# The gate matmuls of a recurrence as four 64x64 quadrants of the array, with a row-swapped copy of their input

## The chip, the cores and the metric

One core of one Trainium2 chip runs the whole kernel in one launch. The metric is the device time of that launch in microseconds (us). A core has a tensor engine (PE; its weight loads are PEld), a vector engine (DVE), a scalar engine (ACT), GpSimd (POOL) and a sync engine (SP); each works through its own list of instructions in order. Data comes and goes by DMA, issued from SP, ACT or POOL.

## The reference

One layer of a hybrid network: windowed attention and a gated linear recurrence side by side, then a mixture of 16 experts. There are 1024 latent tokens and 256 context tokens, 1280 in all. The part that matters here is the recurrence on 512 channels, in both directions of time (d = 0, 1):

```python
def block_diag_linear(x, w, b):            # 8 blocks of 64 x 64
    xb = x.reshape(x.shape[:-1] + (LRU_BLOCKS, LRU_BLOCK_DIM))
    return jnp.einsum('blnd,nde->blne', xb, w).reshape(x.shape) + b

def lru_coeffs(xc, w_r, b_r, w_i, b_i, lam):
    r = jax.nn.sigmoid(block_diag_linear(xc, w_r, b_r).astype(jnp.float32))
    i = jax.nn.sigmoid(block_diag_linear(xc, w_i, b_i).astype(jnp.float32))
    log_a = -LRU_C * r * jax.nn.softplus(-lam.astype(jnp.float32))
    a = jnp.exp(log_a)
    mult = jnp.sqrt(-jnp.expm1(2.0 * log_a))
    return a, mult * i * xc.astype(jnp.float32)
```

`xc` is the input after a width-4 convolution in time. The two gates r and i are the subject: each is a product with a block-diagonal matrix whose blocks are 64x64. Then h[t] = a[t] h[t-1] + b[t] is scanned forwards and backwards, and both are added.

## The kernel before

The stages follow one another: modulation vectors and the normalised input, transposed; projections for keys, values and the recurrence's input; the recurrence; a gate branch and the stacks of the keys; attention by blocks of 128 queries, with output projection and router of the block before; routing; 16 experts, whose weights stream from memory. Everything is float32; large matmuls are split into two float32r parts, the gates' matmuls are plain float32, which PE runs as two passes for each matmul of the program.

In the recurrence, channels lie on the 128 partitions and tokens in a row. The 512 channels are four channel tiles, t = 3, 2, 1, 0, of two 64-channel blocks each. `XR` (lines 359 to 361) holds five slots of [128, 1286]: `XR[0]` is a tile of its own, `XR0` (`xr_655` in the lists of instructions), the other four are parts of one tile (`xr`). `conv(t)` (line 467) reads slot t and writes slot t + 1, in the order 3, 2, 1, 0; so the last convolution, `conv(0)`, reads `XR[0]`, and after it that slot is free until `k_stack` (line 561) uses it as scratch.

`gate_weights(t)` (line 457) clears a [128, 2, 2, 128] tile and loads two 64x64 blocks for each gate and direction onto its diagonal. `lru_tile(t)` (line 480) then does, for each direction and gate, one matmul of 256 columns into a PSUM tile `pgatec` and two of 512 columns into `pgate`, and ACT takes them through tanh (the sigmoid) into a `gate` tile; four such tiles exist. ACT computes exp and tanh of the r gates, after a table load their square root; DVE multiplies and scans (lines 503 to 517). The next tile's first tanh writes into a `gate` tile that the scans have read (line 511).

Between the tiles' steps stand five steps each of the query projection (line 547: `proj`, 24 matmuls of 256 columns, with an ACT copy `qb` behind each). A scheduler puts the instructions of each engine in order ahead of time by its own estimate of when each is ready; the order is then fixed. PSUM is handed out by tags: `pS` has two buffers of 1024 columns, `pO` two single ones of 512 in turn.

Of the kernel before, what the change touches and what calls it, by code (L numbers as in the profile page):

```python
# [8 lines left out]
F32 = mybir.dt.float32  # L9
# [9 lines left out]
D = 1024  # L19
# [3 lines left out]
KT = 8  # L23
# [25 lines left out]
def _body(tc, nc, A, out, dbg, top):  # L49
# [35 lines left out]
    def act(*a, **kw):  # L85
        """an activation whose table set matters: these keep their order on the engine"""
        if last_act[0] is None:
            i = nc.scalar.activation(*a, **kw)
        else:
            with tc.issue_after(last_act[0].ins):  # L90
                i = nc.scalar.activation(*a, **kw)  # L91
        last_act[0] = i
        return i
# [4 lines left out]
    def warm(n, after=None):  # L98
        """keeps the tensor engine's clock up while it waits"""
# [52 lines left out]
    # softplus(-lam) = max(-lam, 0) + log1p(exp(-|lam|)); log1p(e) = 2 atanh(e / (2 + e))  # L152
# [22 lines left out]
    # sigmoid(z + b) = (1 + tanh(z / 2 + b / 2)) / 2  # L175
# [18 lines left out]
    def ada_chunk(n):  # L194
        """[4 groups x (16 rows of c, 16 of c_ctx), 512] of columns n*512.., in SBUF"""
# [15 lines left out]
    gcol = const.tile([128, 40], F32, name="gcol")       # g1, sh2, sc2, g2, (1 + sc2) * norm2_g  # L211

    def ada_col(n):
        """half of one of g1, sh2, sc2, g2 as columns; the half before is finished first"""
# [40 lines left out]
    def projT(hi, lo, segs):  # L255
        """channel rows: [128 channels, tokens]"""
# [8 lines left out]
    AB = const.tile([128, 2, 8, 2], F32, name="ab")      # (scale, shift), k tile, (lat, ctx)  # L265
    a0 = pool(S_a0, "a0", 2)
    a0x = pool(S_a0, "a0x", 6)
    xT = a0.tile([128, KT, 768], F32, name="xT", bufs=1)      # [ctx 256 | lat 512]
# [24 lines left out]
    def ada_half(h):  # L293
        """scale and shift of half of the channels"""
# [64 lines left out]
    XR14 = pxr.tile([128, 4, NT + 6], F32, name="xr")    # slots 1 to 4; slot 0  # L359
    XR0 = pxr.tile([128, NT + 6], F32, name="xr0")  # L360
    XR = [XR0] + [XR14[:, i] for i in range(4)]
    XC0, XL0 = 0, NCTX + 3                               # [2 | ctx | 1 | 2 | lat | 1]
# [9 lines left out]
    def rope_tables(nm, after=None):  # L372
        """weights of the norm; cos and sin tables with them folded in"""
# [16 lines left out]
    def proj(wg, tt):  # L390
        """token rows: [128 tokens, 256 columns]"""
# [9 lines left out]
    def norm_rope(x, nh, b, tabs_):  # L401
        """x: [128, nh, 64], in place; b: latent block, or None (no rope)"""
# [54 lines left out]
    def gate_weights(t):  # L457
        """block-diagonal [128, (gate, direction), 128] of the channel tile"""
        WG = pl.tile([128, 2, 2, 128], F32, name="wg", bufs=2)
        nc.vector.memset(WG, 0.0)  # L460
        for g, nm in ((0, "lru_w_r"), (1, "lru_w_i")):
            for s in range(2):
                nc.gpsimd.dma_start(WG[s * 64:(s + 1) * 64, g, :, s * 64:(s + 1) * 64],
                                    A[nm][0, :, 2 * t + s].rearrange("d i j -> i d j"))
        return WG

    def conv(t):
        """into slot t + 1, whose input is used up"""
# [11 lines left out]
    def lru_tile(t):  # L480
# [4 lines left out]
        R, I, As = [], [], []  # L485
        for d in range(2):
            for gi, nm, lst in ((0, "b_r", R), (1, "b_i", I)):
                g = pl.tile([128, NT], F32, name="gate", bufs=4)
                ps = pS("pgate")
                po = pO("pgatec")[:, :256]  # L490
                mm(po, WG[:, gi, d, :], xc[:, 0:256], True, True)
                for hh in range(2):
                    mm(ps[:, hh * 512:(hh + 1) * 512], WG[:, gi, d, :], xc[:, 256 + hh * 512:768 + hh * 512], True, True)
                act(g[:, 0:256], po, AF.Tanh, scale=0.5, bias=hb[:, gi, d * 4 + t:d * 4 + t + 1])
                act(g[:, 256:NT], ps, AF.Tanh, scale=0.5, bias=hb[:, gi, d * 4 + t:d * 4 + t + 1])
# [35 lines left out]
    # the router with the second norm's scale in its rows, and its shift's share as a row  # L531
# [75 lines left out]
    S_wo, S_wr, S_cs, S_att = (ExitStack() for _ in range(4))  # L607
    WO = []                                              # (hi, lo) of the attention's rows, of the recurrence's rows
# [27 lines left out]
    def q_stack(b):  # L636
        """[128 (hi, lo), head, 128]; heads 2i: (hi, lo), heads 2i + 1: (lo, hi)"""
# [11 lines left out]
    def scores(b, kv, i, qst):  # L649
        """heads kv * 4 + i and kv * 4 + 2 + i of 128 queries: negated scores, then their exponentials"""  # L650
# [5 lines left out]
        # keys: the window, then the context; for the last block the other way round  # L656
# [38 lines left out]
    def attn_out(b, kv, i, pe, ktiles, mx):  # L695
# [20 lines left out]
        # [(head pair, d), (head of the pair, query)]  # L716
        nc.scalar.activation(QB[b][:, kv * 256 + i * 128:kv * 256 + (i + 1) * 128], po, AF.Copy)

    y7 = QBQ[1].rearrange("p a b -> p (a b)")[:, 0:D]         # the last block's share of the recurrence, over queries used up
# [522 lines left out]
```

## Time and profile before

| | |
|---|---|
| timed runs | 1186.73, 1188.15 and 1192.13 us; median 1188.15 |
| span of the profiled execution, first to last instruction | 1185.1 us; no time of its own is listed, the median of the timed runs lies 3.05 us above it |
| PE | 1091.7 us busy, 92% |
| DVE | 946.1 us, 80% |
| ACT | 792.2 us, 67% |
| POOL | 148.6 us, 13% |
| chain that ended last | PE 68%, DVE 12%, issue 7%, ACT 7%, DMA 4% |
| TensorE clock granted, mean of the span | 0.972 |

All rows below are of this one execution. Times count from the first instruction. A busy PE is a modelled figure: matmuls are pipelined, and a matmul's listed duration is longer than the distance to the next one. The rate of matmuls is read from the starts. The recurrence with the steps between it lies at about 175 to 294 us of the span.

### The profile page before, as it was taken

Reading aid. Unit: us, or ns where it says so; the run is one execution under the profiler, and the core shown is the slowest. Engines: PE = TensorE matmul, PEld = TensorE weight load, DVE = VectorE, ACT = ScalarE, POOL = GpSimd, SP = SyncE. Lnnn points to the kernel's source line nnn. Section 1 sums busy time; section 2 is a strip of 40 time slices with the busy share of each in tenths; the row PEclk is TensorE's granted clock in tenths of the full one; section 3 lists DMA queues with packets and bytes.
Section 4 is the critical chain, followed back from the end, with each engine's and each line's share of the span. In section 5 each row is a group of like instructions: output and inputs, shape, how many; then the busy total and the mean of one; then the engine's idle time right before and its main releaser. Section 6 shows DMA issues by size and latency. Waiting matters only on the chain.

```text
span 1185.1 us, 17663 instructions
## 1 busy us (share of the span) xinstructions
PE 1091.7 (92%) x6481; PEld 876.0 (74%) x6481; DVE 946.1 (80%) x1577; ACT 792.2 (67%) x1159; POOL 148.6 (13%) x216
## 2 busy tenths in 40 slices
PE   3889999899799999999299999999999999999996
PEld 1568787667678888877187888888888888887774
DVE  3664557678795585867988999999999999989885
ACT  3652127666385666664268888888888888887873
POOL 2031110111300000000010111011111011110001
PEclk9999999899889999999699999999999999999998
DMA  9857720102141112116889999999999999999932
GB/s 293 293 175 239 236 64 5 40 1 69 37 108 54 55 54 89 55 54 235 334 300 342 342 382 399 382 391 388 384 381 402 383 394 380 383 377 355 359 101 36
DMA packets 97678, 277.14 MB, mean 234 GB/s; under 512 B 6060, under 2 KB 38088, under 8 KB 97592
## 3 DMA queue, kind: packets, MB, share of 16 engines
q1 hardware_dynamic: 90944, 255.87, 57.7%
q0 software_dynamic: 6000, 20.01, 6.8%
q8 instruction: 51, 0.84, 0.3%
q14 instruction: 35, 0.29, 0.1%
q10 hardware_dynamic: 648, 0.13, 0.1%
HBM read 259.21 MB, written 16.79 MB: 233 GB/s over the span
## 4 chain that ended last, share of the span: by engine, by line
PE 68%; DVE 12%; issue 7%; ACT 7%; DMA 4%; POOL 1%; SPq 0%; POOLq 0%; ACTq 0%; DVEq 0%
PE pu L96 14%; PE pg L96 14%; PE pd L96 13%; PE py L96 7%; PE pxr L96 3%; PE pav L713 3%; PE pscore L96 3%; PE pPT L703 3%; DVE mlo L1066 2%; DMA wada<-in_w_ada_dram 2%; ACT gate L91 2%; PE pproj L96 1%; PE pada L203 1%; PE pT L1107 1%; DVE gate L507 1%
## 5 line engine op out<-in xcount | busy, mean ns | idle before, releaser
L1066 DVE TENSOR_TENSOR mlo<-mraw,mhi 128x1024 fp32r<-128x1024 f32 x384 | 448.1, 1217 | 24.5 <-ACT mhi L1063 23.1
L1063 ACT ACTIVATE mhi<-mraw 128x1024 fp32r<-128x1024 f32 x384 | 397.7, 1064 | 75.4 <-PE pg L96 29.0
L96 PE MATMUL pg<-mlo,xsh 128*128 128x512 f32 x256 | 81.9, 401 | 1.4 <-DVE mlo L1066 1.4
L96 PE MATMUL pg<-mhi,xsh 128*128 128x512 f32 x256 | 80.9, 397 | 0.4 <-ACT xsh L1117 0.3
L96 PE MATMUL pu<-mlo,xsh 128*128 128x512 f32 x256 | 80.2, 394 | 0.8 <-DVE mlo L1066 0.5
L96 PE MATMUL pu<-mhi,xsh 128*128 128x512 f32 x256 | 80.8, 390 | 0.0
L96 PE MATMUL pg<-mhi,xsl 128*128 128x512 f32 x256 | 80.4, 395 | 0.0
L96 PE MATMUL pu<-mhi,xsl 128*128 128x512 f32 x256 | 79.1, 390 | 0.0
L96 PE MATMUL pd<-mlo,hdh 128*128 128x512 f32 x240 | 76.0, 398 | 2.4 <-DVE mlo L1066 2.4
L96 PE MATMUL pd<-mhi,hdh 128*128 128x512 f32 x240 | 76.3, 399 | 0.0
L96 PE MATMUL pd<-mhi,hdl 128*128 128x512 f32 x240 | 74.2, 390 | 0.0
L1156 POOL DMA_INDIRECT out_dram<-ys,idx x16 | 49.8, 3113 | 164.2 <-DVE ys L1154 164.2
L1094 POOL DMA_INDIRECT xs<-xh_dram,idx x16 | 21.4, 1335 | 373.0 <-ACT mhi L1063 317.2
L1116 ACT ACTIVATE xs<-pT,gcol 128x128 f32<-128x128 f32 x124 | 46.9, 462 | 26.2 <-PE pT L1107 26.2
L91 ACT ACTIVATE sc<-sc,mx 128x641 f32<-128x641 f32 (+1 forms) x64 | 50.9, 798 | 15.7 <-DVE mx L677 15.7
L96 PE MATMUL pproj<-wlo,hh 128*128 128x256 f32 x192 | 55.5, 289 | 4.4 <-DVE wlo L243 4.4
L677 DVE CUSTOM_DVE_ANT_0 sc<-pscore,kn,nsink 128x640 f32<-128x640 f32 (+1 forms) x64 | 53.4, 842 | 6.0 <-PE pscore L96 5.8
L96 PE MATMUL pproj<-whi,hh 128*128 128x256 f32 x192 | 57.5, 300 | 0.6 <-ACT gate L91 0.6
L709 ACT ACTIVATE pt<-pPT 128x512 f32<-128x512 f32 (+1 forms) x88 | 44.0, 533 | 18.7 <-PE pPT L703 17.6
L96 PEld LDWEIGHTS pu<-mlo,xsh 128*128 128x128 f32 x256 | 47.1, 188 | 12.6 <-DVE mlo L1066 3.5
L96 PEld LDWEIGHTS pg<-mhi,xsl 128*128 128x128 f32 x256 | 48.6, 190 | 10.6
L96 PEld LDWEIGHTS pg<-mlo,xsh 128*128 128x128 f32 x256 | 46.2, 189 | 13.5 <-DVE mlo L1066 4.6
(329 smaller groups left out, 2444.7 us busy)
## 6 DMA issues: line engine op xcount, KB each, us to landing
mraw<-in_w_gate_dram SPq DMA_DIRECT2D x64, 1024.0 KB, 7.6
mraw<-in_w_up_dram SPq DMA_DIRECT2D x64, 1024.0 KB, 9.3
mraw<-in_w_down_dram SPq DMA_DIRECT2D x63, 1024.0 KB, 9.0
wada<-in_w_ada_dram SPq DMA_DIRECT2D x48, 512.0 KB, 5.8
win<-in_w_in_dram SPq DMA_DIRECT2D x7, 1024.0 KB, 5.4
xt<-in_x_dram SPq DMA_DIRECT2D x8, 512.0 KB, 4.3
xa<-in_x_dram SPq DMA_DIRECT2D x8, 512.0 KB, 3.8
out_dram<-xa SPq DMA_DIRECT2D x8, 512.0 KB, 2.7
```

The source lines that it names most:

```text
L91: i = nc.scalar.activation(*a, **kw)
L96: nc.tensor.matmul(o, l, r, start=start, stop=stop)
L203: nc.tensor.matmul(po[32 * j:32 * j + 32, q * 256:(q + 1) * 256], cst[:, half * 4 + j, :], w[:, j, :], start=(half == 0), stop=(half == 1) ...
L677: nc.vector.tensor_tensor_reduce(out=sb[:, :ntot], in0=ps[:, n0:n0 + ntot], in1=mk, scale=-0.125, scalar=nsink[:, h:h + 1], op0=OP.add, op ...
L703: nc.tensor.transpose(p[:, 2 * j + s, :], pe[s][:, (j0 + j) * 128:(j0 + j + 1) * 128], ident)
L709: nc.scalar.activation(dst, src, AF.Copy)
L713: nc.tensor.matmul(po[s * 64:(s + 1) * 64, :], V[:, kt, kv * 64:(kv + 1) * 64], pt[:, j, s], start=(j == 0), stop=(j == nk - 1), skip_grou ...
L1063: nc.scalar.activation(hi, raw[:, j], AF.Copy)
L1066: nc.vector.tensor_tensor(lo, raw[:, j], hi, op=OP.subtract)
L1094: g = nc.gpsimd.indirect_dma_start(out=xs, out_offset=None, in_=xh_dram, in_offset=bass.IndirectOffsetOnAxis(ap=idx[:, :1], axis=0))
L1116: nc.scalar.activation(xf[:, k], p[:, i], AF.Identity, scale=A_, bias=B_)
L1156: nc.gpsimd.indirect_dma_start(out=out_rows, out_offset=bass.IndirectOffsetOnAxis(ap=idx[:, :1], axis=0), in_=ys, in_offset=None, compute_ ...
```

## The change

The weights of a channel tile are no longer laid out as a 128x128 block-diagonal matrix with zeros. The tile `wg` is now [128, 2, 2, 64]: the r gate's blocks lie in partitions 0 to 63, the i gate's in 64 to 127. A matmul takes a 64x64 block at one of four places of the array, (gate, half of the output channels); its input must lie on the gate's 64 partitions. For the half of the channels whose input lies on the other 64 partitions there is a copy `xsw` of the tile's input with the halves of the partitions exchanged. It is written by two DMAs from POOL's queue, in the slot `XR[0]`.

Names in the diff: `xc` is the convolved input of the tile, `hd` the 64-channel block, `gi` the gate, `tile_position` the first row and column in the array.

```diff
     def gate_weights(t):
-        WG = pl.tile([128, 2, 2, 128], F32, name="wg", bufs=2)
-        nc.vector.memset(WG, 0.0)
+        WG = pl.tile([128, 2, 2, 64], F32, name="wg", bufs=2)
         for g, nm in ((0, "lru_w_r"), (1, "lru_w_i")):
             for s in range(2):
-                nc.gpsimd.dma_start(WG[s * 64:(s + 1) * 64, g, :, s * 64:(s + 1) * 64],
-                                    A[nm][0, :, 2 * t + s].rearrange("d i j -> i d j"))
+                nc.gpsimd.dma_start(WG[g * 64:(g + 1) * 64, s], A[nm][0, :, 2 * t + s].rearrange("d i j -> i d j"))
         return WG
 
+    xsw = XR0[:, 0:NT]
...
         xc = XR[t + 1][:, 0:NT]
         R, I, As = [], [], []
+        for h in range(2):
+            nc.gpsimd.dma_start(xsw[h * 64:(h + 1) * 64], xc[(1 - h) * 64:(2 - h) * 64])
         for d in range(2):
-            for gi, nm, lst in ((0, "b_r", R), (1, "b_i", I)):
+            ps = [pS("pgate") for _ in range(2)]
+            po = [pO("pgatec")[:, :256] for _ in range(2)]
+            for outs, c0, n in ((po, 0, 256), ([p_[:, 0:512] for p_ in ps], 256, 512), ([p_[:, 512:1024] for p_ in ps], 768, 512)):
+                for hd in range(2):
+                    for gi in range(2):
+                        r = slice(gi * 64, (gi + 1) * 64)
+                        src = xc if hd == gi else xsw
+                        nc.tensor.matmul(outs[gi][hd * 64:(hd + 1) * 64, :], WG[r, hd, d, :], src[r, c0:c0 + n],
+                                         start=True, stop=True, skip_group_check=True, tile_position=(gi * 64, hd * 64))
+            for gi, lst in ((0, R), (1, I)):
                 g = pl.tile([128, NT], F32, name="gate", bufs=4)
-                ps = pS("pgate")
-                po = pO("pgatec")[:, :256]
-                mm(po, WG[:, gi, d, :], xc[:, 0:256], True, True)
-                for hh in range(2):
-                    mm(ps[:, hh * 512:(hh + 1) * 512], WG[:, gi, d, :], xc[:, 256 + hh * 512:768 + hh * 512], True, True)
-                act(g[:, 0:256], po, AF.Tanh, scale=0.5, bias=hb[:, gi, d * 4 + t:d * 4 + t + 1])
-                act(g[:, 256:NT], ps, AF.Tanh, scale=0.5, bias=hb[:, gi, d * 4 + t:d * 4 + t + 1])
+                act(g[:, 0:256], po[gi], AF.Tanh, scale=0.5, bias=hb[:, gi, d * 4 + t:d * 4 + t + 1])
+                act(g[:, 256:NT], ps[gi], AF.Tanh, scale=0.5, bias=hb[:, gi, d * 4 + t:d * 4 + t + 1])
                 lst.append(g)
```

What the scheduler makes of it is shown at three places. The first is PE at the first channel tile, right behind `pbrow`; here its first direction, before (`pgatec_1721` with `pgate_1720` is one gate, `pgatec_1729` with `pgate_1728` the other):

```order
L96 MATMUL pgatec_1721<-xr_654,wg_1485 128x256 [waits DMASW3_49,DMASW2_49,DVE_49]
L96 MATMUL pgate_1720<-xr_654,wg_1485 128x512 [waits Activation_49]
L96 MATMUL pgate_1720<-xr_654,wg_1485 128x512
L96 MATMUL pgatec_1729<-xr_654,wg_1485 128x256 [waits DMASW5_49,DMASW4_49,DVE_49]
L96 MATMUL pgate_1728<-xr_654,wg_1485 128x512 [waits Activation_49]
L96 MATMUL pgate_1728<-xr_654,wg_1485 128x512
```

And the same direction now (`xr0_655` is the exchanged copy; 1721 and 1719 belong to the gate r, 1722 and 1720 to the gate i):

```order
L497 MATMUL pgatec_1721<-xr_654,wg_1485 64x256 [waits DMASW2_49]
L497 MATMUL pgate_1719<-xr_654,wg_1485 64x512 [waits Activation_49]
L497 MATMUL pgatec_1721<-xr0_655,wg_1485 64x256 [waits DMASW3_49,DMASW2_49]
L497 MATMUL pgate_1719<-xr0_655,wg_1485 64x512 [waits Activation_49]
L497 MATMUL pgate_1719<-xr_654,wg_1485 64x512
L497 MATMUL pgatec_1722<-xr0_655,wg_1485 64x256 [waits DMASW4_49,DMASW3_49,DVE_49]
L497 MATMUL pgatec_1722<-xr_654,wg_1485 64x256 [waits DMASW5_49]
L497 MATMUL pgate_1720<-xr0_655,wg_1485 64x512 [waits PE_49]
L497 MATMUL pgate_1720<-xr_654,wg_1485 64x512
L497 MATMUL pgate_1720<-xr0_655,wg_1485 64x512
L497 MATMUL pgate_1719<-xr0_655,wg_1485 64x512
L497 MATMUL pgate_1720<-xr_654,wg_1485 64x512
```

Six matmuls became twelve, the two gates are interleaved, and the third instruction waits for the first exchanged copy, the sixth for the second. In both orders the second direction stands right behind, and only behind that the query projections (`pproj`).

The second place is POOL, from the first weights of the gates on (`wg`: weights; `xr_655<-xr`: the copies). Before, and behind it now:

```order
L463 DMA wg<-in_lru_w_r_dram 64x2x64 x2
L463 DMA wg<-in_lru_w_i_dram 64x2x64 x2
L463 DMA wg<-in_lru_w_r_dram 64x2x64 x2
L463 DMA wg<-in_lru_w_i_dram 64x2x64 x2
L463 DMA wg<-in_lru_w_r_dram 64x2x64 x2
```

```order
L462 DMA wg<-in_lru_w_i_dram 64x2x64 x2
L488 DMA xr_655<-xr 64x1280 x3
L462 DMA wg<-in_lru_w_r_dram 64x2x64 x2
L462 DMA wg<-in_lru_w_i_dram 64x2x64 x2
L488 DMA xr_655<-xr 64x1280 x2
```

Two of the first three copies are the first channel tile's; they wait for the last instruction of `conv(0)`, which reads the slot that they write. The others wait for the matmuls of the tile before.

The third place is ACT ahead of the third channel tile (t = 1). Before:

```order
L552 ACTIVATE qb<-pproj 128x256
L404 ACTIVATE nrsq<-qb 128x512
L552 ACTIVATE qb<-pproj 128x256
L91 ACT_TABLE_LOAD
L91 ACTIVATE gate<-pgatec,hb 128x256
```

And now:

```order
L559 ACTIVATE qb<-pproj 128x256
L404 ACTIVATE nrsq<-qb 128x512
L559 ACTIVATE qb<-pproj 128x256
L404 ACTIVATE nrsq<-qb 128x512
L91 ACT_TABLE_LOAD
```

A second `nrsq` (a square for the norm of the queries) stands ahead of the table load; before, it stood among the tanh of that tile. In the first three tiles one more `qb` copy than before stands among the four exponentials. The four clears of `wg` are gone from DVE.

## Rows read from the trace of the kernel before

**Rows 1.** Windows: stretch; its length, then busy us (instructions) by engine, clock, DMA.
```profile
175.00:203.00 28.00, 28.00 (x163) 21.75 (x163) 20.20 (x19) 17.91 (x22) 2.37 (x4) 1.00 0.02 6
203.00:235.00 32.00, 27.10 (x150) 21.45 (x148) 21.77 (x16) 20.32 (x25) 3.48 (x6) 0.89 0.12 37
```

**Rows 2.** Chain that ended last, 173 to 292 us: start, us, what.
```profile
173.48 1.71 PE pbrow L96 x16
...
193.44 2.89 DVE gate L507 x2
...
203.24 1.49 ACT gate L91 x2
...
218.47 2.89 DVE gate L507 x2
...
228.65 5.07 PE pproj L96 x22
...
260.48 1.49 ACT gate L91 x2
...
288.83 2.34 DVE gate L515
```

**Rows 3.** Timeline of DVE: start, us, engine, line, operation, form, count.
```profile
176.43 0.81 DVE L471 TENSOR_SCALAR xr<-xr,sm 128x1024 f32<-128x1024 f32 x1
177.28 3.92 DVE L474 SCALAR_TENSOR_TENSOR xr<-xr,sm,xr 128x1024 f32<-128x1024 f32 x3
...
227.40 1.20 DVE L243 TENSOR_TENSOR wlo<-win,whi 128x1024 fp32r<-128x1024 f32 x1
```

**Rows 4.** Timeline of ACT; in brackets idle time before, and what ended it.
```profile
182.78 0.47 ACT L91 ACTIVATE gate<-pgatec,hb 128x256 f32<-128x256 f32 x1
183.91 1.11 ACT L91 ACTIVATE gate<-pgate,hb 128x1024 f32<-128x1024 f32 x1 [0.67 <-PE pgate L96]
...
189.11 0.36 ACT L552 ACTIVATE qb<-pproj 128x256 f32<-128x256 f32 x1
...
208.94 1.12 ACT L91 ACTIVATE gate<-pgate,hb 128x1024 f32<-128x1024 f32 x1 [0.67 <-PE pgate L96]
...
231.82 0.63 ACT L404 ACTIVATE nrsq<-qb 128x512 f32<-128x512 f32 x1
...
234.15 1.28 ACT L91 ACT_TABLE_LOAD   x1
```

**Rows 5.** Timeline of PE: passes of the gates; the first projection after a wait.
```profile
175.54 1.88 PE L96 MATMUL pgate<-xr,wg 128*128 128x512 f32 x4
177.26 0.59 PE L96 MATMUL pgatec<-xr,wg 128*128 128x256 f32 x2
...
228.65 0.58 PE L96 MATMUL pproj<-wlo,hh 128*128 128x256 f32 x1 [4.40 <-DVE wlo L243]
```

**Rows 6.** DMA issues of POOL: KB each, median us to landing.
```profile
xr<-row_dram POOLq DMA_DIRECT2D x1, 512.0 KB, 3.8
...
wg<-in_lru_w_r_dram POOLq DMA_DIRECT2D x8, 32.0 KB, 2.0
...
xs<-xh_dram,idx POOLq DMA_INDIRECT x16, 7.7
```

**Rows 7.** Timeline of POOL: two DMAs issued one after the other.
```profile
184.84 1.19 POOL L463 DMA_DIRECT2D wg<-in_lru_w_r_dram  x2 [28.58 <-DVE wg L460]
```

**Rows 8.** Windows around that wait of PE; the clock is third from the end.
```profile
224.00:229.00 5.00, 0.60 (x2) 0.35 (x2) 5.00 (x5) 0.00 (x0) 0.00 (x0) 0.87 0.00 0
229.00:234.00 5.00, 5.00 (x24) 4.84 (x23) 4.71 (x4) 1.27 (x3) 0.19 (x1) 0.50 0.64 210
234.00:239.00 5.00, 3.75 (x11) 1.79 (x10) 3.11 (x6) 4.97 (x8) 1.67 (x1) 0.95 0.00 2
```

**Rows 9.** Chain: a round of matmuls on four column strips of the array.
```profile
121.74 1.86 PE pada L203 x32
```

**Rows 10.** One line's instructions, weight loads of 64 columns: ns min/median/max.
```profile
L713 PEld LDWEIGHTS pav<-pt,v x608: 132/137/137, 334.3 to 554.6; 128*64 128x64 f32 x152
```

## The prediction

> **What bounds the kernel now.** I read the windows over the recurrence first, then the chain of waits through it, then the timelines of DVE, ACT and PE at the places that the chain names. The windows show PE busy for the whole of 175 to 203 us and for 27.1 of the next 32 us, DVE and ACT for about two thirds [rows 1]. Taken alone this says that PE is the limit. The chain says otherwise [rows 2]. From 193 us on it runs in a ring: the square roots on ACT release DVE's multiplications (193.44), the scan behind them releases the next tile's tanh (203.24), its exponentials and roots release DVE again (218.47), and so to the last scan (288.83). PE is on it at the start (`pbrow`, the head of its list, 173.48) and where half of a projection's weights come late (228.65). There PE has waited 4.40 us for DVE's `wlo` [rows 5], which stands behind the scan in DVE's list [rows 3]. In the rest of the stretch PE fills the time with projections that nobody on the ring waits for. So a time that is taken off PE there is worth nothing by itself, and a time that is added to a tile's gates, from their input to the last tanh, moves everything behind it.
>
> **The first tile's gates wait for a copy.** Before, the gates of tile 3 need `conv(3)`, long done; they start when PE comes to them at about 175, and the last tanh ends at 183.91 + 1.11 = 185.0 [rows 4]. Now three quarters of PE's first list of gates stand behind the exchanged copy, which is written into the slot that `conv(0)` reads. `conv(0)` is the last convolution: one instruction from 176.43, three from 177.28 that take 3.92, so its end is 181.2 [rows 3]. What is queued behind the waiting matmul is all of PE: both directions of the gates and then the projections. Step by step:
> - POOL issues two copies of 320 KB at about 0.6 each, since two take 1.19 [rows 7]; the second goes out at 181.9. No row shows a transfer within the on-chip memory. A load of 32 KB lands after 2.0, one of 512 KB after 3.8, an indirect one of 512 KB beside the weight stream after 7.7 [rows 6]. The DMA engines are idle here (0.02 of their time [rows 1]), so I take 3.8: landed at 185.7. The ends are 183.9 and 189.6.
> - Behind the second copy seven matmuls are left in the first direction. A full-array pass of 512 columns takes 0.43, since the four from 175.54 last until the next start at 177.26 [rows 5]; one of 256 columns takes half, 0.215, and a program's matmul is two passes. I let different quadrants run together and the same quadrant one after the other, in the list's order: one step of 0.43 and two of 0.86, in all 2.15.
> - PE has then idled some nine us. After the idle 4.40 us before 228.65 the granted clock was 0.50, and it rose again at about 234.5, 5.8 us after the work came back (0.95 in the last window) [rows 5, 8]. So I take the lower level, 1.2 GHz, for this direction: 4.3 instead of 2.15, and 0.2 until ACT sees the end, 190.2.
> - ACT drains r (1.11, then 191.3) and i (0.47 + 1.11, to 192.8) [rows 4]. Only then is i's PSUM buffer free for the second direction, and in the new list r's last quadrant stands behind i's first ones. So two steps of 0.86 follow: 194.7. Then 1.11 + 0.47 + 1.11: the last tanh ends at 197.4.
>
> That is 12.4 later than 185.0. With the early landing it is 10.6, with the late one 16.3; without the drop of the clock 2.15 less.
>
> The Trainium skill ("DMA: Bandwidth & Descriptors", Anatomy of one DMA) gives 2.0 us plus the bytes at 436 KB per us for a DMA of this queue, which for 327,680 bytes is an estimate of 2.75 us. By it the landing is 1.05 earlier and the result about 1202.5.
>
> **The other tiles.** Their copies go out as soon as PE has finished the tile before (194.7 for tile 2, whose tanh then start near 216); they hide behind the exponentials, roots and scans, and if that cover were gone they would cost their 4 to 5 us each. The gates themselves lengthen on ACT. Before, tile 2's four pairs of tanh take 203.24 to 208.94 + 1.12, 6.8 us [rows 2, 4], with PE half a step ahead. Now a direction's two gates finish together: ACT drains r and i by 3.2 us after its start, r of the second direction is complete two steps of 0.86 later at 5.1, and 2.7 more end at 7.8. That is +1.0. In tile 1, where no scan holds up the second drain, the same sum gives 7.4, +0.6. In tile 0 the third tanh waits for DVE as before: nothing.
>
> **Moved on ACT.** One more `qb` copy of 0.36 [rows 4] among the exponentials of tiles 3, 2 and 1, 0.3 each with its overlap: +0.9. A `nrsq` of 0.63 ahead of the table load at 234.15 [rows 4]: +0.6.
>
> **At no cost.** The four clears of `wg` and two scratch copies that move to tile 0 lie in DVE's idle third [rows 1]. Eight transposes of the first key stack move behind the first two products of the gate branch; at a quarter of 0.43 each they are 0.9 us, and I expect them in PE's wait for ACT there; without that cover they cost 0.9. What PE saves is at best half of its gate time: 16 gates of four passes of 0.43 and two of 0.215 make 34.4, so 17.2. In the list as it is, with the same quadrant twice in a row at places, it is less, and it goes into waits.
>
> **Sum.** 12.4 + 1.0 + 0.6 + 0.9 + 0.6 = 15.5. The profiled span of 1185.1 becomes 1200.6; the median of the timed runs lies 3.05 above the span, so 1203.5 after rounding. Behind the last scan everything follows in the same order, and the experts' weights are requested behind stores, not at fixed times; I see nothing that gives it back.
>
> **A rule on quadrants that share rows.** Rows 9 show four column strips that take their input from the same 128 rows: 32 passes of 256 columns in 1.86 us, where one after the other would be 32 x 0.215 = 6.9. So matmuls and weight loads of strips with the same rows do run together [rows 9]. The Trainium skill ("TensorE: Matmul & The Clock Gate", Part 3, the mechanism) says that a weight load overlaps a running matmul only if its group of rows is another one. The trace does not bear that out here. By the rule two loads of 0.13 [rows 10] would be exposed in each of nine matmul steps on the path, 2.4 us, and the sum would be 1206.
>
> **Rivals.**
> - PE is the limit after all: PE is full in the windows [rows 1]. Then the saved 17.2 us come off, 1171. Against it stand the chain, and the waits of DVE and ACT in the same stretch. Chance 0.07.
> - The quadrants do not run together: strips of columns are shown [rows 9], strips of rows are not. Each direction is then 20 slots of 0.43. In tile 3 twelve slots remain behind the copy instead of five (7.7 us with the clock's rise, for 4.3), and the second direction has 16 slots, 6.9, in place of 3.4 behind r's drain; tiles 2 and 1 lose 3.5 each, tile 0 1.8. In all 15.7 more: 1219. It decides from the point where two halves of the rows exclude each other; if only those do and column strips run together, about 6 more, 1210, which the range holds. Chance 0.08 for the full price.
> - The delay is taken up: the ring has about 7 us of waiting ahead of tile 1, from the scan's end near 227 to the table load at 234.15 [rows 3, 4]. If the projections there came earlier, and the copies landed after 2.0 without a drop of the clock, 15.5 - 7 - 1.8 - 2.15 leaves 4.5: 1192.5, inside 0.5%. Against it: what holds tile 1 is `wlo` behind the scan, which moves along. Chance 0.08.
>
> **How the numbers follow.** The forecast has 0.77. Its own ends are 1199.5 (early copy and full clock) and 1213 (late copy, two strips at a time in part). The range reaches lower and takes in the halfway cases of the third rival: 1196 to 1213. What this kernel's measurement can tell from no change is about 0.5%, 6 us. Slower by more: 0.77 + 0.08 = 0.85, less 0.02 for combinations that end below 1194: 0.83. Within: 0.09. Faster: 0.08.
>
> **What would show it.** In the new profile the third gate matmul of tile 3 starts near 185 with a wait for a DMA on it; the clock is at the lower level around 181 to 191; DVE's multiplications of tile 3 start near 206, not at 193.44 [rows 2]; the tanh of tile 2 span 7.8 us; the last scan starts near 304. Gate passes of different quadrants start within some ns of each other. If the first tile's last tanh ends before 190, or the last scan starts within 6 us of its old place, the argument is wrong; if passes of different row halves never overlap, the second rival holds.

## The result and the profile after

The changed kernel is slower. Its median is 1208.19 us (1205.64 to 1208.93, four runs) against 1189.37 us (1186.73 to 1192.13, four runs) for the kernel before; the ratio is 1.0157 with a 95% interval of 1.0136 to 1.0178, which is 18.7 us (16.2 to 21.2). The forecast was 1203.5 us, with a range of 1196 to 1213. The profiled execution spans 1206.0 us, 20.9 more than before; the mean granted clock is 0.958, it was 0.972.

Three words are used below. A drain is ACT's tanh out of a PSUM buffer, which frees the buffer. A pair is the two drains of one gate, 256 and 1024 columns. A tile's block is its four pairs, eight tanh, from the first start to the last end.

The windows of the changed kernel over the same two stretches of time as [rows 1], and one more (columns as there; the granted clock is third from the end):

```profile
175.00:203.00 28.00, 18.20 (x118) 12.26 (x118) 9.47 (x9) 11.25 (x15) 4.51 (x8) 0.82 0.22 52
203.00:235.00 32.00, 28.85 (x203) 21.74 (x202) 15.85 (x11) 21.89 (x26) 3.48 (x6) 0.89 0.11 26
218.00:224.00 6.00, 5.68 (x22) 2.21 (x23) 3.10 (x3) 2.42 (x5) 0.09 (x1) 0.50 0.00 0
```

In the first stretch PE was busy all of the time; now it stands still for ten of 28 us, DVE has half of its former work in it and ACT two thirds. The third line is a stretch in which the gates of tile 2 run, with the clock at the lower level. In the kernel before, the clock is at 1.00 where its gates of tile 2 run:

```profile
199.00:207.00 8.00, 7.50 (x39) 5.31 (x38) 7.58 (x6) 5.20 (x8) 0.00 (x0) 1.00 0.00 1
207.00:213.00 6.00, 6.00 (x41) 5.02 (x41) 2.92 (x3) 5.30 (x6) 2.37 (x4) 1.00 0.06 19
```

The chain of waits shows the same steps as [rows 2], later (start, us, what):

```profile
182.65 3.35 DMA xr<-xr
...
206.98 2.89 DVE gate L514 x2
...
216.78 1.49 ACT gate L91 x2
...
234.72 2.90 DVE gate L514 x2
...
269.69 2.89 DVE gate L514 x2
...
298.27 2.89 DVE gate L514 x2
...
308.32 2.35 DVE gate L522
```

The transfer is new on it. The lines on DVE answer to 193.44 and 218.47 of [rows 2] and to 250.68 and 278.78 for tiles 1 and 0; the last scan to 288.83. So the delay is 13.5 us at tile 3, 16.3 at tile 2, 19.0 at tile 1, 19.5 at tile 0 and at the last scan. Of the first number 0.85 is older than the change's work: the last convolution ends 0.85 later in this execution (182.05 for 181.2 in [rows 3]). PE's timeline (start, us, engine, line, operation, form, count; in brackets idle time before, and what ended it) shows both halves of the story:

```profile
186.05 0.69 PE L497 MATMUL pgatec<-xr,wg 64*64 64x256 f32 x1 [8.60 <-DMA xr<-xr]
...
211.59 0.65 PE L497 MATMUL pgatec<-xr,wg 64*64 64x256 f32 x4
...
212.51 1.99 PE L497 MATMUL pgate<-xr,wg 64*64 64x512 f32 x10
217.31 0.66 PE L497 MATMUL pgatec<-xr,wg 64*64 64x256 f32 x4 [2.81 <-ACT gate L91]
218.31 1.11 PE L497 MATMUL pgate<-xr,wg 64*64 64x512 f32 x1 [0.34 <-ACT gate L91]
218.94 0.69 PE L497 MATMUL pgatec<-xr,wg 64*64 64x256 f32 x2
218.95 1.11 PE L497 MATMUL pgate<-xr,wg 64*64 64x512 f32 x1
```

The first line is the third gate matmul of tile 3; it waited 8.60 us for the copy (forecast: near 185), and the clock was at the lower level from 180.3 to 190.5 (forecast: around 181 to 191). From 211.59 to 214.50 twenty of the 24 passes of tile 2's first direction run at the upper clock (the other four start at 207.52). Then PE has nothing to do for 2.81 us until ACT has drained a buffer, and when the second direction starts, the clock falls: the same 512 columns that took 0.59 in the list now take 1.11. ACT pays for it (its timeline in tile 2, third and fourth pair of tanh):

```profile
219.79 0.47 ACT L91 ACTIVATE gate<-pgatec,hb 128x256 f32<-128x256 f32 x1
223.70 1.11 ACT L91 ACTIVATE gate<-pgate,hb 128x1024 f32<-128x1024 f32 x1 [3.43 <-PE pgate L497]
...
225.07 1.12 ACT L91 ACTIVATE gate<-pgate,hb 128x1024 f32<-128x1024 f32 x1
```

The wait of 3.43 answers to 0.67 in [rows 4] (208.94). Behind the last scan the same instructions start 18.6 us later from 330 to 560 us, and 20.4 later from 640 us on. The last 1.8 fall into the routing, where PE's clock is low for 30.7 us in this execution and was for 27.3 before. The quadrants alone don't decide that: of the runs below, e9 with the old gates has 30.7, and e4, e5, e6 and e10 with quadrants have 27.3. The timed difference of 18.7 us is near the 18.6 ahead of the routing.

### The profile page after: what moved, and what is told of

Read it like the earlier page. It is cut to its first block, busy times and chain, and to the rows that moved or that the text cites. A ratio compares the mean times of both kernels' runs of the same rounds, so it can differ in the third digit from the quotient of the medians.

```text
span 1206.0 us, 17854 instructions
## 1 busy us (share of the span) xinstructions
PE 1097.9 (91%) x6577; PEld 873.9 (72%) x6577; DVE 944.5 (78%) x1573; ACT 792.5 (66%) x1159; POOL 154.5 (13%) x224
## 4 chain that ended last, share of the span: by engine, by line
PE 68%; DVE 12%; ACT 7%; issue 7%; DMA 4%; POOL 1%; SPq 0%; POOLq 0%; ACTq 0%; DVEq 0%
PE pu L96 14%; PE pg L96 13%; PE pd L96 12%; PE py L96 7%; PE pxr L96 3%; PE pav L720 3%; PE pscore L96 3%; PE pPT L710 3%; ACT gate L91 2%; DVE mlo L1073 2%; DMA wada<-in_w_ada_dram 2%; PE pgate L497 2%; PE pproj L96 1%; PE pada L203 1%; PE pT L1114 1%
## 5 line engine op out<-in xcount | busy, mean ns | idle before, releaser
L96 PEld LDWEIGHTS pg<-mlo,xsh 128*128 128x128 f32 x256 | 46.6, 191 | 13.6 <-DVE mlo L1073 4.4
L96 PEld LDWEIGHTS pu<-mlo,xsh 128*128 128x128 f32 x256 | 47.1, 188 | 12.6 <-DVE mlo L1073 3.0
```

The lines of the kernel that those rows point to most:

```text
L96: nc.tensor.matmul(o, l, r, start=start, stop=stop)
```

## The experiments

All were timed against the kernel before on the same chip, in five rounds. The table gives the ratio to the kernel before with its interval, the length of each tile's block on ACT, the starts of tile 3's multiplications and of the last scan on DVE, and the length of the stage, all in us from each run's own profile. The stage is counted from the end of the last convolution to the start of the last scan, because that convolution ends between 181.1 and 184.1 us in these executions, and the starts carry this along. e1 to e11 are short for the labels; there is no e8.

| run | ratio (95% interval) | tile 3 | tile 2 | tile 1 | tile 0 | mult. of tile 3 | last scan | stage |
|---|---|---|---|---|---|---|---|---|
| before | | 9.29 | 6.82 | 6.82 | 9.08 | 193.44 | 288.83 | 107.63 |
| changed | 1.0157 (1.0136 to 1.0178) | 11.24 | 9.41 | 9.14 | 9.55 | 206.98 | 308.32 | 126.27 |
| e1 copy in own tile | 1.0069 (1.0057 to 1.0081) | 8.69 | 9.28 | 8.49 | 9.10 | 194.70 | 295.16 | 112.63 |
| e2 wait alone | 1.0185 (1.0170 to 1.0200) | 10.27 | 6.82 | 6.83 | 7.03 | 206.56 | 300.10 | 119.04 |
| e3 r first | 1.0119 (1.0104 to 1.0133) | 12.32 | 6.02 | 7.50 | 11.31 | 209.98 | 307.78 | 123.68 |
| e4 warm | 1.0183 (1.0165 to 1.0200) | 11.95 | 7.66 | 7.40 | 15.65 | 209.01 | 314.29 | 130.89 |
| e5 clock | 1.0133 (1.0112 to 1.0155) | 10.28 | 7.65 | 7.39 | 9.82 | 205.77 | 303.83 | 121.54 |
| e6 all three | 1.0030 (1.0018 to 1.0043) | 7.35 | 8.69 | 7.10 | 12.67 | 194.28 | 294.73 | 111.16 |
| e7 wait, first tile | 1.0105 (1.0087 to 1.0123) | 11.04 | 6.82 | 6.83 | 9.08 | 208.65 | 303.36 | 120.93 |
| e9 split earlier | 0.9978 (0.9964 to 0.9991) | 9.29 | 6.82 | 10.52 | 9.08 | 193.37 | 285.62 | 104.48 |
| e10 mended | 0.9981 (0.9966 to 0.9996) | 7.35 | 6.28 | 6.92 | 9.11 | 193.06 | 288.04 | 105.70 |
| e11 mended, split earlier | 0.9974 (0.9962 to 0.9987) | 7.35 | 6.29 | 10.52 | 9.08 | 194.02 | 285.75 | 102.45 |

**e1: the copy in a tile of its own.** Against the changed kernel:

```diff
-    xsw = XR0[:, 0:NT]
+        xsw = pl.tile([128, NT], F32, name="xsw")
```

> The changed kernel with the exchanged copy in a tile of its own instead of the input's slot 0; nothing else is edited. Theory (the copy's slot makes the first tile wait, and the clock falls in the other tiles): the first tile's copies no longer wait for the last convolution, its last tanh ends near 184 us instead of 198.4, its multiplications start near 193 instead of 207; tiles 2, 1 and 0 keep their added 2.6, 2.7 and 0.5 us. Time about 1195 us (1193 to 1198). Rival (the quadrant form itself or the transfers cost it): 1204 us or more.

Measured: 1196.37 us. ACT's timeline, the last tanh of tile 3 and the third pair of tile 2:

```profile
185.06 1.12 ACT L91 ACTIVATE gate<-pgate,hb 128x1024 f32<-128x1024 f32 x1
...
211.31 1.12 ACT L91 ACTIVATE gate<-pgate,hb 128x1024 f32<-128x1024 f32 x1 [3.32 <-PE pgate L496]
```

The last tanh of tile 3 ends at 186.2, near the 185.0 of the kernel before (this run too is 1.3 late from the stages ahead). Tile 2's wait for PE is still there, 3.32. From one tile's multiplications to the next's it takes 27.6 us to tile 2 (25.0 before), 34.7 to tile 1 (32.2) and 28.1 to tile 0 (28.1). The stage is 13.6 us shorter than in the changed kernel and 5.0 longer than before, which is the loss in tiles 2 and 1. By the ratios the wait for the slot is worth some 10 us, and 8 remain. The 3 that the stage doesn't explain lie behind it: in this execution 1.6 come at a stretch of low clock in attention (3.4 us from 514.8) and 2.1 in the routing (30.7 us low). e9, with the gates of the kernel before, shows such stretches too (3.4 us from 504.9; 30.7), so they are not put down to the quadrants; what brings them was not tried.

**e2 and e7: the wait without the quadrants.** Against the kernel before (e7 has both lines for t == 3 alone):

```diff
+        xsw = XR0[:, 0:NT]
+        for h in range(2):
+            nc.gpsimd.dma_start(xsw[h * 64:(h + 1) * 64], xc[(1 - h) * 64:(2 - h) * 64])
...
+                src = xsw if d == 0 and gi == 0 else xc
```

> The kernel before, with its block-diagonal gates, plus the two copies per tile into slot 0; the reset gate's matmuls of the first direction read the copy in place of the input, so that they wait for it (those gates are computed from exchanged rows). Theory: the wait alone gives the first tile's part: last tanh near 197.5 us instead of 185.0, multiplications of tile 3 near 206 instead of 193.4; tiles 2, 1 and 0 take as long as before, since PE keeps its full gate time and does not fall idle ahead of them. Time about 1201 us (1199 to 1204). Rival (the quadrants themselves cost most): within 4 us of the kernel before, 1189 to 1193.

Measured: 1209.52 us, eight more than expected. The stage itself does what was expected: the multiplications of tile 3 start at 206.56, the tanh of tiles 2 and 1 take 6.82 and 6.83 as before, and the last scan comes 11.3 late (tile 0's block is 2.1 shorter here). Of the rest, 9.3 us are lost right behind the stage: the same instructions start 11.3 late at 310 us and 20.6 late from 320 us on (times of the kernel before). Waits of PE behind the recurrence, in this run and then in the kernel before (who waited, for whom: us in total, times, longest):

```profile
PE pT L573 <- DVE kl L576: 11.2, 2, 9.1
```

```profile
PE pT L569 <- DVE kl L572: 3.4, 1, 3.4
```

Slot 0 is also the scratch of the key stack. With copies in all four tiles it comes free only at the last one, the key stack's first transposes move behind the recurrence, and in this order PE meets a wait of 9.1 us there. That was read from the trace, so e7 tested it: copies and wait in the first tile alone.

> The kernel before, with the copies and the wait in the first tile only (the three matmuls of gate r, first direction, tile 3 read the copy, so that gate is computed from exchanged rows); afterwards slot 0 is free for the key stack as before. Theory: the first tile's multiplications start 12.5 to 13 us later, nothing else changes: about 1200.5 us (1198.5 to 1202). Rival (the 1209.5 of the run with copies in all tiles came from the wait and not from the key stack, whose transposes the held slot pushed behind the stage): 1205 us or more.

Measured: 1200.76 us; the key stack's wait is back at 3.4 us. The chain of e7 around the copy (start, us, what) and a window:

```profile
183.56 4.27 DMA xr<-xr
...
208.65 1.49 DVE gate L511
```

```profile
188.00:194.00 6.00, 6.00 (x9) 2.95 (x10) 0.90 (x2) 1.86 (x3) 0.00 (x0) 0.55 0.01 3
```

The wait alone, with PE's full-array matmuls behind it, costs 12.5 us by the ratio (10.3 to 14.6), and no other tile's block is longer. In the profile the stage is 13.3 longer: 14.0 at tile 3, of which 0.7 comes back ahead of tile 1 (16.30 us from tile 2's multiplications to tile 1's first tanh, for 16.97 before). Here too the clock is at the lower level when the waiting matmuls start.

**e3: gate r ahead of gate i.** A list of steps, chained in this order, for the second direction:

```diff
+            if d in (1,):
+                steps = [(0,0,0),(0,1,0),(1,0,0),(1,1,0),(2,0,0),(2,1,0),(0,0,1),(0,1,1),(1,0,1),(1,1,1),(2,0,1),(2,1,1)]
```

The triples are segment of columns, half of the output channels, gate.

> The changed kernel; in the second direction of each tile all quadrant matmuls of gate r stand ahead of those of gate i on PE. Theory: r is complete after 2.15 us of its own at the upper clock (4.3 at the lower) instead of at the end, and its drain runs beside i's matmuls; the tanh of a tile shorten by about 1 us in tiles 3, 2 and 1 and by half of that in tile 0: time about 1205 us (1203.5 to 1206.5). Rival (only the clock counts, not the order): within 1 us of the changed kernel, 1207 to 1209.

Measured: 1202.74 us, more gain than expected and below the expected range. Tile 2's block is 6.02, shorter than the 6.82 before. The window over it and its third pair of tanh on ACT:

```profile
218.00:224.00 6.00, 5.37 (x41) 2.54 (x41) 4.95 (x5) 4.88 (x7) 0.00 (x0) 1.00 0.00 1
```

```profile
224.26 1.11 ACT L91 ACTIVATE gate<-pgate,hb 128x1024 f32<-128x1024 f32 x1 [0.30 <-PE pgate L502]
```

Two things changed at once: the order, and with it the place of the first direction, which the scheduler now put behind the projections, directly ahead of the second. PE had no gap there, and the clock stayed at 1.00. So this run doesn't tell order and clock apart; e4 and e5 do. In the profiled execution tile 3's multiplications start 3.0 later than in the changed kernel although the median is lower: 2.05 of that comes from the stages ahead, and the block of tile 3, at 0.50 until 204.9, is 1.1 longer. In tile 0 the new order cost 1.8: a square of the query norm slipped in front of the last tanh and waited for DVE.

**e4: the gap of PE filled.** Matmuls on the identity, on a spare bank, chained between the directions; the order is otherwise the changed kernel's:

```diff
+            n_warm = {2: 20, 1: 14, 0: 20}.get(t, 0)
+            if d == 1 and n_warm:
+                wp = pT("warm")
+                for _ in range(n_warm):
...
+                        wi = nc.tensor.matmul(wp[:, 0, :], ident, ident, start=True, stop=True)
```

> The changed kernel with idle-time matmuls (20, 14 and 20 of 128 x 128 on a spare bank) between the two directions of tiles 2, 1 and 0; the order on PE is otherwise the same. Theory: the granted clock stays at the upper level while these tiles' second directions run, their matmuls take half as long (3.4 us from the first drain instead of 5.4), and the tanh of tiles 2 and 1 shorten from 9.4 and 9.2 us to about 7.7, tile 0 by 0.5: time about 1204 us (1202.5 to 1205.5). Rival (the coarser order alone lengthens them, 1.0 and 0.6 as predicted, and the rest is elsewhere): no change, 1207 to 1209.

Measured: 1210.78 us, no gain in the total; but tiles 2 and 1 did what the theory said. Tile 2's window, and on ACT the third pair of tiles 2 and 0:

```profile
218.50:224.00 5.50, 5.50 (x50) 3.65 (x49) 4.63 (x3) 3.65 (x7) 0.00 (x0) 1.00 0.02 4
```

```profile
223.99 1.12 ACT L91 ACTIVATE gate<-pgate,hb 128x1024 f32<-128x1024 f32 x1 [1.69 <-PE pgate L510]
...
290.66 0.63 ACT L404 ACTIVATE nrsq<-qb 128x512 f32<-128x512 f32 x1 [3.06 <-DVE nrss L406]
291.20 1.10 ACT L91 ACTIVATE gate<-pgate,hb 128x1024 f32<-128x1024 f32 x1
```

The clock is 1.00, the wait for PE falls from 3.43 to 1.69, and the blocks from 9.41 and 9.14 to 7.66 and 7.40. What was gained was lost in tile 0: its filling changed the order on ACT, and two squares stood ahead of the third pair's second tanh and waited for DVE; its block took 15.65 for 9.55. The expectation for the total failed by this, and not in tiles 2 and 1, which the clock was to shorten; e5 leaves tile 0 alone.

**e5: the clock held in tiles 3, 2 and 1.** As e4, with 18 and 12 matmuls in tiles 2 and 1, 36 ahead of tile 3's gates, and none in tile 0.

> The changed kernel with idle-time matmuls of 128 x 128 on a spare bank in three places: 36 ahead of the first tile's gates (while they wait for the copy), 18 and 12 between the two directions of tiles 2 and 1; nothing in tile 0. Theory: the clock stays at the upper level there; the first direction of tile 3 takes 2.7 us after the copy's landing instead of 5.4 (2.2 to 2.6 less), the tanh of tiles 2 and 1 take 7.7 and 7.4 us instead of 9.4 and 9.1. Time about 1202.5 us (1201 to 1204). Rival (the clock is only a companion, the order alone decides): 1206 us or more.

Measured: 1202.97 us, as the theory said, and its span of 1200.8 is 5.2 below the changed kernel's. The interval of its ratio still touches the changed kernel's, so the trace has to carry it. Tile 2's window and the third pair on ACT there:

```profile
216.00:221.00 5.00, 5.00 (x41) 2.89 (x40) 3.89 (x3) 3.16 (x6) 0.04 (x1) 1.00 0.00 0
```

```profile
220.75 1.12 ACT L91 ACTIVATE gate<-pgate,hb 128x1024 f32<-128x1024 f32 x1 [1.69 <-PE pgate L513]
```

Blocks of 7.65 and 7.39, the same as in e4. In tile 3 the first direction took 4.0 us from the first copy's landing to ACT's drain, 5.4 in the changed kernel: 1.4 less, not the 2.2 to 2.6 expected, because at the upper clock the second copy, which lands later than the first (187.75 for 186.25), is waited for once more. The stage is 4.7 shorter than in the changed kernel, which is these three pieces (1.4, 1.8 and 1.75) less 0.3 in tile 0.

**e6 and e10: everything undone but the quadrants.** e6 joins e1, e3's order in tiles 3, 2 and 1, and the filling of tiles 2 and 1.

> The changed kernel with all three remedies: the copy in a tile of its own, gate r's quadrants ahead of gate i's in the second direction of tiles 3, 2 and 1, and 18 and 12 idle-time matmuls between the directions of tiles 2 and 1. Theory (these are all the causes): the tanh of tiles 2 and 1 take about 6.0 to 6.2 us, less than the 6.8 of the kernel before; against the run with the copy's own tile 3.2 and 2.3 us come off, and the extra projection copies among the exponentials are gone with the new order. Time about 1190.5 us (1188.5 to 1192.5), the kernel before within some 3 us. Rival (quadrants cost something not yet seen): 1194 us or more.

Measured: 1191.48 us, the expected total, but not by the expected parts: tile 2 took 8.69 instead of 6.0, tile 0 12.67. PE's timeline and ACT's in tile 0 say why:

```profile
203.66 4.29 PE L497 MATMUL warm<-ident 128*128 128x128 f32 x36
```

```profile
272.45 0.63 ACT L404 ACTIVATE nrsq<-qb 128x512 f32<-128x512 f32 x1 [2.94 <-DVE nrss L406]
```

In the new order the filling started only at 203.66 and stood in the way until 207.9, two us behind the first drain (205.56); and a square waited for DVE inside tile 0's third pair, much as in e3. e10 takes both away (no filling in tile 2, 8 matmuls in tile 1, the fifth square chained behind the last tanh).

> The run with all three remedies, mended where its trace showed its own losses: no idle-time matmuls in tile 2 (there they ended 2 us after the drain that they should bridge) and 8 instead of 12 in tile 1; and the fifth square of the query norms held behind the last tanh of tile 0, where it stood ahead of the third tanh and kept it waiting for DVE. Theory: tanh blocks of tiles 2 and 1 about 6.0 and 6.3 us (8.7 and 7.1 in that run, 6.8 before), tile 0 about 9.1 (12.7 in that run): 6.9 us less than that run, 1184.6 us (1183 to 1187.5), so about 3 us below the kernel before. Rival (the quadrants are worth nothing on the ring): 1188 or more.

Measured: 1185.96 us, 0.9981 of the kernel before (0.9966 to 0.9996). With the copy out of the way, gate r first and no gap on PE ahead of tile 2's second direction the kernel with quadrants is no longer slower, it is about 2 us faster. The block of tile 2 is 6.28 for 6.82, though tile 1's is 6.92 where 6.3 was expected. The stage is 1.9 shorter than before: 1.5 by tile 3, whose last tanh ends 0.4 earlier although the last convolution ends 1.1 later, and 0.5 by tile 2. The square that is held back doesn't bring it, since tile 0's block is 9.11 for 9.08. The kernel before was not timed with the new order of the steps beside the gates, so the 2 us are the quadrants' together with that order. The timelines on ACT and PE of tile 2:

```profile
206.38 1.11 ACT L91 ACTIVATE gate<-pgate,hb 128x1024 f32<-128x1024 f32 x1
207.39 0.47 ACT L91 ACTIVATE gate<-pgatec,hb 128x256 f32<-128x256 f32 x1
208.03 1.12 ACT L91 ACTIVATE gate<-pgate,hb 128x1024 f32<-128x1024 f32 x1 [0.18 <-PE pgate L513]
```

```profile
204.39 0.64 PE L513 MATMUL pgate<-xr,wg 64*64 64x512 f32 x1 [0.36 <-ACT gate L91]
204.40 0.64 PE L513 MATMUL pgate<-xsw,wg 64*64 64x512 f32 x1
204.87 0.59 PE L513 MATMUL pgate<-xr,wg 64*64 64x512 f32 x1
204.88 0.59 PE L513 MATMUL pgate<-xsw,wg 64*64 64x512 f32 x1
...
205.30 0.59 PE L513 MATMUL pgate<-xr,wg 64*64 64x512 f32 x1
205.31 0.59 PE L513 MATMUL pgate<-xsw,wg 64*64 64x512 f32 x1
```

ACT's longest wait for PE is 0.18 in these lines, in place of 3.43.

**e9 and e11: the wait that the chain showed from the start.** [Rows 5] have 4.40 us in which PE waits for `wlo`, which stands behind a scan. e9 is the kernel before with the split of the second group of weights requested ahead of tile 2:

```diff
+        if (0, 5)[i % 2] == 5 * i:
+            wnext = split_group(load_raw(i * 256))
         lru_tile(t)
...
-                wg = split_group(load_raw(g * 256))
+                wg = wnext
```

> The kernel before with one edit: the split of the second group of projection weights is requested ahead of tile 2 of the recurrence instead of behind it, so that its last part on DVE stands ahead of that tile's last scan. Theory (the stage is a ring, and tile 1 waits in it for these weights): PE's wait of 4.4 us goes, tile 1 starts about 3 us earlier although the split's 1.2 us each now stand among DVE's multiplications: about 1185 us (1182 to 1187). Rival (the wait is not on the path, or the split takes as much as it gives): 1187 to 1190.

Measured: 1185.39 us, 0.9978. Tile 1's first tanh and its third instruction there, on ACT:

```profile
228.55 0.47 ACT L91 ACTIVATE gate<-pgatec,hb 128x256 f32<-128x256 f32 x1
...
232.62 0.47 ACT L91 ACTIVATE gate<-pgatec,hb 128x256 f32<-128x256 f32 x1 [2.59 <-DVE gate L515]
```

The tile starts at 228.55 instead of 235.44, but its second gate then waits for the scan of tile 2 (2.59), and its block takes 10.52 for 6.82, so that 3.2 of the 6.9 us are kept.

> The mended run with the split of the second group of projection weights requested ahead of tile 2, as in the run with that edit alone. Theory (both act on different pieces of the ring and add up): 2.7 us less than the mended run, 1182 us (1180 to 1185), below the run with that edit alone (1185.4). Rival (tile 1's wait is the same one): 1184.5 or more.

Measured: 1184.52 us, 0.9974 (0.9962 to 0.9987), which both the theory's range and the rival's bound hold, so the time doesn't decide. The stage does, for the theory: it is 5.2 us shorter than before, in e9 3.2 and in e10 1.9, so the two gains add up there. Tile 1's block is 10.52 in e9 and e11, but the scan of tile 2 that sets it has itself moved. In the total only 3.1 us (1.5 to 4.5) arrive; in this execution stretches of low clock lie behind the stage as in e9 (3.4 us from 505.5; 30.7 us from 567.0), and whether they take the rest was not tried. e9, e10 and e11 all beat both kernels, the one before by 2 to 3 us; which of the three is best lies within their intervals.

## Why the prediction was right, and where its sum was off

**The bound was right.** The stage is a ring, and PE's time is worth little in it by itself: PE's busy time from 175 to 203 fell from 28.0 to 18.2 us and the kernel became slower. The first rival (PE is the limit, 17.2 us come off) is out by this and by e1, where the quadrants run without the wait and still lose 8 us. "Worth nothing" was a little too strong: in tile 3, ahead of the ring, ACT waits for PE's gates in the kernel before too, and in e10 the stage is 1.9 us shorter than before.

**That the range held the time is in part luck.** The forecast was 4.7 us too low. The range reached to 1213 for a copy that lands late and for quadrants that run two at a time; neither came, and what did come, the clock in tiles 2 and 1, was not what that room was for. A smaller error had the other sign: the median was put 3.05 us above the span, but here 1207.85 stands against 1206.0, 1.85, and the executions of the kernel before that were timed with the experiments show 1.8 to 1.9. So the profiled 1185.1 was a fast execution.

**The first tile was right in its sum.** Forecast +12.4, measured 198.44 - 185.03 = 13.4, less the 0.85 that came from ahead: 12.6. Its pieces were off in both directions and happen to cancel. The transfers of tile 3 took 3.4 and 4.3 us from issue to landing; their median is 3.8, the row that was chosen from [rows 6]. But the second, for which 185.7 was forecast, landed at 187.48: 0.85 from ahead, 0.4 by its issue and 0.5 by its length. From there to ACT's drain (191.41) it took 3.9 us, where 4.3 and 0.2 were forecast; most of it ran at the lower clock, which rose at 190.5. The second direction took from 193.9 (drain of i) to 195.95, 2.1 us, where two steps made 1.7. The lower clock cost 1.4 us in this tile by e5, where the prediction priced it at 2.15. e7 gives 12.5 by the ratio without any quadrant. The landing of the two (of all instructions on `xr` from 182 to 190 us), and the row for all eight copies, which stands beside [rows 6]:

```profile
DMA to landing us min/median/max: 3.4/3.8/4.3
```

```profile
xr<-xr POOLq DMA_DIRECT2D x8, 320.0 KB, 3.3
```

By the formula of the Trainium skill ("DMA: Bandwidth & Descriptors", Anatomy of one DMA) the estimate was 2.75 us; the trace has 3.3 in the median of the eight, and decides.

**The term that failed is "The other tiles".** It gave tile 2 +1.0, tile 1 +0.6, tile 0 nothing. Measured: 9.41 - 6.82 = 2.6, 9.14 - 6.82 = 2.3, 9.55 - 9.08 = 0.5. As a term for the order it was well sized: with the clock held, e4 and e5 show 7.66 - 6.82 = 0.84 and 7.40 - 6.82 = 0.58. What it left out is the clock, 1.75 us in each of the two tiles. The prediction let the time that PE saves "go into waits" at no cost, and charged the lower clock to the one long wait of tile 3; but the saved time becomes a gap on PE just ahead of the second direction, 2.81 us in tile 2, 2.01 in tile 1 and 2.71 in tile 0, and each time the clock fell in the gap or right behind it (at 217.8, 252.0 and 279.3). The rows for a gap of 4.40 us and its price were in hand [rows 5, 8]; they were not applied to the shorter gaps that the change itself makes. The length of the gap alone doesn't tell whether the clock falls: in the kernel before PE stands still for 1.98 us from 291.64 and the clock stays at 1.00, while in e1 it fell behind gaps of 1.76 and 1.67 us (at 207.6 and 241.8).

```profile
288.00:295.00 7.00, 5.02 (x23) 3.83 (x22) 6.02 (x5) 3.74 (x5) 0.73 (x2) 1.00 0.23 62
```

The Trainium skill ("TensorE: Matmul & The Clock Gate", Part 1, HAM oscillation) describes a kernel whose compute falls to the lower clock again after each wait for a transfer; here the waits are for ACT's drains, and the window of tile 2 at 0.50 agrees with it.

**The two small terms on ACT were too large.** The extra `qb` copies were put at 0.9; from the last tanh to the multiplications it takes 8.54 us for 8.41 in three tiles, together 0.4. The square ahead of the table load was put at 0.6; from tile 2's multiplications to tile 1's first tanh it takes 17.28 for 16.97, so 0.3.

So the ring's own part is 12.6 + 2.6 + 2.3 + 0.5 + 0.4 + 0.3 = 18.7 where 15.5 were forecast; with the 0.85 from ahead it is the 19.5 of the last scan. About 0.9 came back ahead of attention, by the starts of the same instructions, where the prediction saw nothing; what gave it back was not followed.

**The second rival is out.** Twenty passes in 2.9 us (211.59 to 214.50) are two fifths of what one after the other would take (8 x 0.215 + 12 x 0.43 = 6.9), and less than the 3.4 of strips of columns that run two at a time. Different halves of the rows overlap: by the order of the list the lines at 218.94 and 218.95 are gate i (rows 64 to 127) and gate r (rows 0 to 63). Nor did the rule on quadrants that share rows cost anything: in e10 the same two quadrants of gate r follow each other every 0.43 us (204.87, 205.30), both on rows 0 to 63, and their loads of 0.13 us start at 204.88, under passes that started at 204.87.

**The third rival** (the delay is taken up ahead of tile 1) is out: from tile 2's multiplications to tile 1's first tanh the delay grew by 0.3 us, and at tile 1's multiplications it is 19.0 for 16.3 at tile 2's.

## What to carry to other kernels

Ask of time saved on an engine that isn't the bound where the gap will lie: on PE gaps of two to three us ahead of work that the ring waits for brought the lower clock here, and cost 1.75 us in each of two tiles, where the quadrants at their best (e10) gained about 2 in the whole kernel. Before a scratch buffer is put into a slot that "is free", list its last reader and its next user on all engines: both made a wait here, one ahead of the stage (12 us) and, in e2, one behind it (9 us). And when a change loses on a ring, the ring's oldest wait is the cheaper place: requesting one split of weights earlier (e9) gave as much as mending everything about the quadrants (e10).

## What the runs showed of the hardware

- The granted clock went to 0.50 in or right behind gaps of PE of 2.0 to 2.8 us, not only of 4.40 or 8.60 us; in e1 it did so behind 1.76 and 1.67 us, and in the kernel before it stayed at 1.00 over 1.98 us. At the lower level a gate pass of 512 columns is then listed at 1.06 to 1.11 us instead of 0.59 to 0.64, and the same quadrant follows itself every 0.85 us instead of 0.43. Filled with matmuls, the same places ran at 1.00 (e4, e5).
- Two copies of 320 KB within the on-chip memory, issued 0.5 us apart from POOL, landed after 3.4 and 4.3 us; in e7 the second took 4.27. Issued 2.9 us apart (tile 2) both took 3.2.
- Matmuls on quadrants of different rows and of different columns started 6 to 13 ns apart, and their weight loads of 0.13 us ran under passes on the same rows (e10), where the same quadrant followed itself every 0.43 us.
